# A two-block transformer layer on one core: attention and RWKV chunk products on zero-padded operands over the whole array

## Chip, cores and metric

One core of one Trainium2 chip runs the whole program. The metric is the device time of one execution in microseconds (us).

## What is computed

The first block runs attention and an RWKV-7 time mix side by side on 256 tokens of width 2048, then `w_out` and a gated FFN; a second block with three other attentions and an FFN follows. What the change touches is the first block's mix:

```python
def rwkv7_step(state, inp):                 # 16 heads of 64, scanned over 256 tokens
    r, w, k, v, a, bb = inp
    sa = jnp.einsum('bhij,bhj->bhi', state, a)
    state = (state * w[:, :, None, :] + sa[..., None] * bb[:, :, None, :]
             + v[..., None] * k[:, :, None, :])
    y = jnp.einsum('bhij,bhj->bhi', state, r)
    return state, y
...
kk = kk / jnp.maximum(jnp.sqrt(jnp.sum(kk * kk, axis=-1, keepdims=True)), 1e-12)   # per head
y = ((y - mu) * lax.rsqrt(var + GN_EPS)).reshape(b, s, RWKV_WIDTH) * ln_w + ln_b    # per head
...
logits = jnp.einsum('bnqrhd,bnkrhd->bnrhqk', qb, kc) * ATTN_SCALE + bias            # dilated attention
```

All inputs, weights and the result are float32.

## The kernel before, in words

Every large projection goes through `lin`: a 512 KB piece of weights is loaded on the SP queue (tile `raw`), ScalarE casts it to a high part `wh` (L333), VectorE subtracts for the low part `wl` (L334), and TensorE does three products per piece and token half, `wh·xh`, `wl·xh` and `wh·xl`, 512 columns wide (in the first projections 256). All of TensorE's products have the line L220 (helper `mm`) or L225 (helper `tr`, transposes), so they are told apart by their tiles.

Between these products the RWKV part is worked off in four groups `g` of four heads (two pairs `p` of two heads `hh`), and 256 tokens are cut into 8 chunks `c` of 32. Per group: `rwkv_pre` (decays; `lora`), `rwkv_keys` (`hs`, `nt`, `sp`: unit keys), `rwkv_rv` (`bn`), `rwkv_pairs` (products within the chunks `D`, transposed keys `BT`, values with tokens on partitions `V`), `solve_T` and `chain`, then `rwkv_out` (`yt` turns Y back to channels on partitions, `g` is the gate).

`solve_T` inverts the chunks' triangular matrices. `D` goes to DRAM and back in another layout (`scN`, `N`, on SP's queue), GpSimd does 31 steps of two operations each (tiles `X`, `T`, L584 and L586), the result goes to DRAM and back (`scT`, `TTx`), and only then can the first T product of that group's `chain` run.

`chain` goes from chunk to chunk: X = N·V + A·S, copied out of PSUM (`Xc`), U = T·X, copied (`UV`), the new state from `BKT`·UV (`S`), and Y = R·S + D·UV. Each float32 product appears as two MATMUL records, a transpose as one. A·S, R·S and the D products address 64 columns of the array, N·V and the T products 64 rows by 64 columns, `V` 64 by 32 and `yt` 128 by 64.

The attention (`attn_quarter`, 4 heads each) transposes q and k (`qkt`), forms logits of heads of 64 channels (`lg`) and works on tiles from a ring of 6 (`aq`). Loads for it and for the groups (`nq`, `toep`, `kB` ...) are issued by GpSimd.

A scheduler in the build fixes each engine's order once; on the chip every engine runs its list in that order, and an instruction that waits holds all behind it on its engine.

Of the kernel before, what the change touches and what calls it, by code (L numbers as in the profile page):

```python
# [19 lines left out]
P = 128  # L20
S = 256
# [76 lines left out]
def constants():  # L98
# [4 lines left out]
    # chunk mask: row (X, hh, t), column (Y, hh, s)  # L103
# [8 lines left out]
    c["selT"] = (np.arange(4)[:, None] == (np.arange(256) // 64)[None, :]).astype(f)  # L112
# [23 lines left out]
def host_arrays(inp):  # L136
    """Layout only: weights in the order of their use, parameters by channel."""
# [48 lines left out]
class Builder:  # L186
# [55 lines left out]
    def rstd(self, ss, n, eps, name):  # L242
        """(ss / n + eps) ** -0.5 for a small tile ss."""
# [16 lines left out]
    def row_rstd(self, ss, name):  # L260
        """Per-token rstd [128, tb] of rows of 2048, from the partial sums of squares."""
# [5 lines left out]
    def split_T(self, src, kts, hi, lo, gain=None, scale=None, tag="rw"):  # L267
        """hi + lo = (natural src(tb, kt) [128 tokens, 128 channels] transposed) * gain(kt)."""
# [31 lines left out]
    def lin(self, wname, bi, xT, evac, kmap=None, ks=None):  # L300
        """One block of columns of x @ w: evac(tb, psum [128 tokens, n]) for both token blocks."""
# [49 lines left out]
class Block1(Builder):  # L351
# [1 line left out]
    def rwkv_consts(self):  # L353
# [4 lines left out]
        self.selT = self.load_const("c_selT", [4, 256], pool)  # L358
# [27 lines left out]
    def slot(self, shape, name):  # L386
        """A tile of up to 2112 bytes per partition from the shared slots."""
# [14 lines left out]
    def nat_evac(self, dst, scale):  # L402
        """Evacuation of a projection block into dst[:, tb, :n], times the tokens' scale."""
# [5 lines left out]
    def shift_mix(self, out, ps, col):  # L409
        """out = ps + (ps of the token before - ps) * mix, [rows, 256]."""  # L410
# [22 lines left out]
    def lora_tanh(self, dst, r0, bias, st):  # L433
        """dst = tanh((bias + low rank) / 2)."""
        ps = self.aux("lora")
        for p in range(2):
            q = 2 * st.g + p
            self.mm(ps[:, p * S:(p + 1) * S], st.lup[r0:r0 + 64, p * P:(p + 1) * P], self.waT[r0:r0 + 64, :])
# [11 lines left out]
    def rwkv_pre(self, g):  # L450
        """What needs the low-rank inputs only: decays and the removal's strength."""
# [4 lines left out]
        st.lup = self.set2("lup", [P, S])  # L456
        nc.sync.dma_start(st.lup, self.A["lup"][:, cs])
        # decays, their inverses, and the products of both within a chunk (entry 0: the empty product)
# [17 lines left out]
        self.lora_tanh(st.a, 64, self.a0h, st)  # L476
        return st

    def rwkv_keys(self, st, natk):
# [4 lines left out]
        # half the removal key, of unit length per head  # L484
# [18 lines left out]
        nT = self.p1.tile([4, S], F32, tag="nT", name=self.nm("nT"))  # L503
        v.tensor_scalar(nT, pn[0:4, 0:S], 0.5, None, op0=ALU.mult)
# [14 lines left out]
    def rwkv_rv(self, st, natr, natv):  # L519
# [8 lines left out]
        # bonus, times v, in place of r  # L528
# [7 lines left out]
    def rwkv_pairs(self, st):  # L536
        """Decayed keys, products within the chunks, operands with tokens on partitions."""
# [22 lines left out]
        for p in range(2):  # L560
            pv = self.aux("V")
# [4 lines left out]
            nc.scalar.copy(st.UV[64:128, 8 * p:8 * p + 8, :], pv[64:128].rearrange("p (a b) -> p a b", a=8))  # L566

    def solve_T(self, st):
        """TTx = ((I - N)^-1)^T of every head and chunk, N the strictly lower products of the removal.

        Partition 32q + (head, chunk) holds the rows 4a + q of T."""
# [17 lines left out]
        r = 64 * (st.g % 2)  # L589
        for hh in range(2):  # L590
            nc.sync.dma_start(self.TTx[r + 32 * hh:r + 32 * hh + 32, :, 32 * hh:32 * hh + 32],
                         self.scT[hh].rearrange("c t s -> t c s"))

    def chain(self, st):
        """From chunk to chunk: X = A S + N_k V, U = T X, the state, and the outputs Y."""
# [10 lines left out]
        for c in range(8):  # L606
            for p in range(2):
                o, cs = 8 * p + c, slice(64 * p, 64 * p + 64)
# [3 lines left out]
            X = self.p1.tile([P, 2, 64], F32, tag="Xc", name=self.nm("Xc"), bufs=2)  # L612
            nc.scalar.copy(X[tr], a2(ch[0:64, 0:128]))
            for p in range(2):
                self.mm(ch[0:64, 128 + 64 * p:192 + 64 * p], self.TTx[tr, 8 * p + c, :], X[tr, p, :])
            v.tensor_copy(UVv[0:64, :, c, :], a2(ch[0:64, 128:256]))
            if c < 7:
                for p in range(2):
                    self.mm(ch[:, 256 + 64 * p:320 + 64 * p], st.BKT[:, 8 * p + c, :], st.UV[:, 8 * p + c, :])
                Sn = self.p1.tile([P, 2, 64], F32, tag="S", name=self.nm("S"), bufs=2)  # L620
                l = lc[:, :, c, :].to_broadcast([P, 2, 64])
            for p in range(2):
                o, ys = 8 * p + c, ch[64:128, 64 * p:64 * p + 64]
# [10 lines left out]

    def rwkv_out(self, st):
        """Group norm per head, back to channels on partitions, bonus and gate; stored for w_out."""
# [15 lines left out]
        gup = self.p1.tile([P, 2, S], F32, tag="gup", name=self.nm("gup"))  # L652
        nc.sync.dma_start(gup[:, 0, :], self.A["gup"][0:P, cs])
        nc.sync.dma_start(gup[0:32, 1, :], self.A["gup"][P:160, cs])
        ps, pg = self.aux("yt"), self.aux("g")
        for p in range(2):
            for c in range(4):
                for hh in range(2):
# [3 lines left out]
            self.mm(pg[:, p * S:(p + 1) * S], gup[:, 0, cs], self.gT[:, 0, :], stop=False)  # L662
            self.mm(pg[:, p * S:(p + 1) * S], gup[0:32, 1, cs], self.gT[0:32, 1, :], start=False)
            nc.scalar.activation(out[:, p, :], ps[:, p * S:(p + 1) * S], AF.Identity,
                                 scale=self.pv("ln_w", 2 * st.g + p), bias=self.pv("ln_b", 2 * st.g + p))
# [640 lines left out]
```

## Time and profile before

| | us |
|---|---|
| three runs | 2868.22, 2868.26, 2871.14 (median 2868.26) |
| profiled execution, span from first to last instruction | 2868.2 |
| TensorE busy with matmuls | 2824.0 (98%), 14032 records |
| VectorE, ScalarE, GpSimd busy | 1728.1, 1540.2, 165.4 |

The profiled execution's own time is its span; it stands within 0.1 us of the median. Records of matmuls overlap in the profile (each one's end is modelled), so what a product costs is read from the starts of neighbouring records, or from the chain of waits, which lays the pieces end to end. The first block's mix fills the first 667 us; after that come the FFNs and the second block, which the change leaves alone.

### The profile page before, as it was taken

The page shows a single profiled execution, that of the slowest core. Times are in us where ns is not written, and L with a number is a line of the kernel's source. Part 1 is how long each engine was busy: PE and PEld are TensorE (multiplying, and loading weights), DVE is VectorE, ACT ScalarE, POOL GpSimd, SP SyncE. Part 2 cuts the span into 40 slices and gives each one's busy share as a digit, 9 for nine tenths or more (in the row PEclk, how much of TensorE's full clock was granted, in tenths as well). Part 3 has the DMA queues.
Part 4 walks back from the last instruction along what each step waited for, and adds up shares of the span by engine and source line. Part 5 has one row for each costly group of instructions (what it writes and reads, how often), then busy time and mean ns, then how long its engine had stood idle before and what let it go on. Part 6 is the DMA issues. An engine that isn't in the chain of part 4 may idle for free.

```text
span 2868.2 us, 40953 instructions
## 1 busy us (share of the span) xinstructions
PE 2824.0 (98%) x14032; PEld 2327.4 (81%) x14032; DVE 1728.1 (60%) x3036; ACT 1540.2 (54%) x2791; POOL 165.4 (6%) x353
## 2 busy tenths in 40 slices
PE   7999999999999999999999999999999999999999
PEld 6877777777888888888888888888888888888887
DVE  5565656646555555555666676656666666667554
ACT  5444446446455454445555665555556666666444
POOL 1044033300000000000000000000000000000000
PEclk9999999999999999999999999999999999999999
DMA  6645446565555555555655545665555555555564
GB/s 215 193 160 153 159 158 202 182 197 191 188 192 186 191 191 189 191 192 187 214 186 173 169 165 191 202 202 195 190 184 186 186 185 185 184 184 190 200 201 167
DMA packets 168481, 534.43 MB, mean 186 GB/s; under 512 B 30853, under 2 KB 35983, under 8 KB 168272
## 3 DMA queue, kind: packets, MB, share of 16 engines
q1 hardware_dynamic: 149220, 487.91, 51.8%
q0 software_dynamic: 7360, 25.28, 2.9%
q10 hardware_dynamic: 11692, 18.63, 1.9%
q8 instruction: 110, 1.80, 0.3%
q14 instruction: 99, 0.81, 0.1%
HBM read 518.07 MB, written 16.82 MB: 186 GB/s over the span
## 4 chain that ended last, share of the span: by engine, by line
PE 93%; DMA 2%; DVE 1%; POOL 1%; ACT 1%; issue 1%; SPq 0%; ACTq 0%; DVEq 0%; POOLq 0%
PE lin L220 85%; PE ch L220 3%; PE tr L225 1%; PE uT L225 1%; POOL T L586 1%; POOL X L584 1%; DMA raw<-in_w_in_dram 1%; DVE wl L334 0%; PE o L220 0%; PE pt L220 0%; PE D L220 0%; PE lg L220 0%; PE V L220 0%; DMA x<-in_x_dram 0%; ACT wh L333 0%
## 5 line engine op out<-in xcount | busy, mean ns | idle before, releaser
L334 DVE TENSOR_TENSOR wl<-raw,wh 128x512 fp32r<-128x512 f32 (+2 forms) x1848 | 1268.4, 689 | 928.3 <-PE lin L220 814.2
L333 ACT CAST wh<-raw 128x512 fp32r<-128x512 f32 (+2 forms) x1848 | 1140.1, 619 | 1119.0 <-PE lin L220 1063.1
L220 PE MATMUL lin<-wl,x2h 128*128 128x512 f32 (+2 forms) x800 | 293.4, 369 | 2.9 <-DVE wl L334 2.9
L220 PE MATMUL lin<-wh,x2l 128*128 128x512 f32 (+2 forms) x800 | 289.4, 364 | 0.0
L220 PE MATMUL lin<-wl,u2h 128*128 128x512 f32 x704 | 281.0, 399 | 0.0
L220 PE MATMUL lin<-wl,hhi 128*128 128x512 f32 x704 | 275.0, 391 | 0.0
L220 PE MATMUL lin<-wh,u2l 128*128 128x512 f32 x704 | 274.3, 390 | 0.0
L220 PE MATMUL lin<-wl,uh 128*128 128x512 f32 x704 | 273.9, 391 | 0.0
L220 PE MATMUL lin<-wh,hlo 128*128 128x512 f32 x704 | 273.9, 389 | 0.0
L220 PE MATMUL lin<-wh,ul 128*128 128x512 f32 x704 | 272.7, 390 | 0.5 <-DVE ul L292 0.5
L220 PE MATMUL lin<-wh,x2h 128*128 128x512 f32 (+2 forms) x800 | 245.0, 365 | 1.6 <-ACT wh L333 1.2
L220 PE MATMUL lin<-wh,uh 128*128 128x512 f32 x704 | 227.6, 391 | 0.9 <-ACT uh L291 0.8
L220 PE MATMUL lin<-wh,u2h 128*128 128x512 f32 x704 | 225.5, 392 | 0.0
L220 PE MATMUL lin<-wh,hhi 128*128 128x512 f32 x704 | 219.9, 389 | 0.0
L220 PE MATMUL lin<-wl,xh 128*128 128x512 f32 (+2 forms) x512 | 188.8, 373 | 3.6 <-DVE wl L334 3.6
L220 PE MATMUL lin<-wh,xl 128*128 128x512 f32 (+2 forms) x512 | 178.3, 352 | 0.0
L220 PE MATMUL lin<-wh,xh 128*128 128x512 f32 (+2 forms) x512 | 156.0, 360 | 20.5 <-ACT wh L333 20.5
L220 PEld LDWEIGHTS lin<-wl,x2h 128*128 128x128 f32 x800 | 150.8, 189 | 29.0 <-DVE wl L334 6.0
L220 PEld LDWEIGHTS lin<-wh,x2h 128*128 128x128 f32 x800 | 147.9, 189 | 26.7 <-ACT wh L333 2.3
L220 PEld LDWEIGHTS lin<-wh,x2l 128*128 128x128 f32 x800 | 150.9, 189 | 22.7
L220 PEld LDWEIGHTS lin<-wh,uh 128*128 128x128 f32 x704 | 132.2, 188 | 29.4 <-ACT uh L291 1.5
L220 PEld LDWEIGHTS lin<-wh,u2h 128*128 128x128 f32 x704 | 132.2, 188 | 27.8
(417 smaller groups left out, 3754.4 us busy)
## 6 DMA issues: line engine op xcount, KB each, us to landing
raw<-in_w_in_dram SPq DMA_DIRECT2D x268, 512.0 KB, 3.8
raw<-in_w_gate_up_dram SPq DMA_DIRECT2D x176, 512.0 KB, 4.3
raw<-in_w_down_dram SPq DMA_DIRECT2D x176, 512.0 KB, 4.2
raw<-in_w_up_dram SPq DMA_DIRECT2D x176, 512.0 KB, 3.2
raw<-in_w_out_dram SPq DMA_DIRECT2D x64, 512.0 KB, 3.7
raw<-in_w_mem_kv_dram SPq DMA_DIRECT2D x16, 512.0 KB, 4.0
raw<-in_w_br_fox_dram SPq DMA_DIRECT2D x12, 512.0 KB, 3.2
raw<-in_w_br_sb_dram SPq DMA_DIRECT2D x12, 512.0 KB, 3.8
```

Source lines behind the costliest of these rows:

```text
L220: self.nc.tensor.matmul(out, lhsT=lhsT, rhs=rhs, start=start, stop=stop)
L225: self.nc.tensor.transpose(out, in_, self.ident[p0:p0 + n, p0:p0 + n])
L333: nc.scalar.copy(wh[:, :m * n], raw[:, cs])
L334: nc.vector.tensor_tensor(wl[:, :m * n], raw[:, cs], wh[:, :m * n].bitcast(F32), op=ALU.subtract)
L584: gp.tensor_tensor(x, T[:, 0:m, u:u + 1].to_broadcast([P, m, n]), N[:, u:u + 1, u + 1:32].to_broadcast([P, m, n]), op=ALU.mult)
L586: gp.tensor_tensor(w, w, x, op=ALU.add)
```

## The change

- `V`: 64 float32 products of 64x32 per group pair become four full 128x128 transposes per group; the copies out go by 32 partitions, four on ScalarE, four on VectorE. The half of `UV` that is not yet known is set to zero by GpSimd.
- `yt`: 16 float32 products per group become four transposes; four ScalarE copies and two VectorE operations take the place of two ScalarE activations.
- `rwkv_keys`: two narrow transposes, a VectorE operation and two products with a 4-row operand (`nt`, `nT`, `sp`) become a ScalarE copy `nr` [128, 512] and four transposes.
- `chain`: A·S and R·S are one product over all 128 columns, N·V comes with a D product over all rows and columns; T·X of both pairs is one product with a block-diagonal 128x128 `TTx`. X and U are copied in halves, one on VectorE and one on ScalarE. GpSimd copies U into `Ux` (rest zero), and D·Ux adds U's part to Y. Every chunk now waits for a GpSimd copy.
- `TTx` is one buffer for all groups (two halves before), filled by four DMAs in place of two; `lup` and `gup` are single zero-padded buffers; `qz` holds q zero-padded per head, one buffer, and the ring `aq` has 5 tiles.

```diff
 # rwkv_keys
-        pn = self.aux("nt")
-        for tb in range(2):
-            self.tr(pn[0:4, tb * P:(tb + 1) * P], nn[:, 4 * tb:4 * tb + 4])
...
+        nr = self.slot([P, 8, 64], "nr")
+        nc.scalar.activation(nr, nn.unsqueeze(2).to_broadcast([P, 8, 64]), AF.Copy, scale=0.5)
...
         for p in range(2):
-            self.mm(ps[:, p * S:(p + 1) * S], self.selT[:, p * P:(p + 1) * P], nT)
+            for tb in range(2):
+                self.tr(ps[:, p * S + tb * P:p * S + (tb + 1) * P], nr[:, tb, p * P:(p + 1) * P])
 # rwkv_pairs
-                for c in range(8):
-                    self.tr0(pv[64 + 32 * hh:96 + 32 * hh, c * 64:(c + 1) * 64],
-                             st.v[64 * hh:64 * hh + 64, p, c * 32:(c + 1) * 32])
+        nc.gpsimd.memset(st.UV[0:64], 0.0)
+        for i in range(4):
+            self.tr(pv[:, i * P:(i + 1) * P], st.v[:, i // 2, (i % 2) * P:(i % 2 + 1) * P])
...
 # solve_T
+        for p in range(2):
+            for hh in range(2):
+                r = slice(64 * p + 32 * hh, 64 * p + 32 * hh + 32)
+                nc.sync.dma_start(self.TTx[r, :, r], self.scT[hh, 8 * p:8 * p + 8].rearrange("c t s -> t c s"))
 # chain, per chunk c
-                self.mm(ch[0:64, cs], D[64:128, o, 0:64], st.UV[64:128, o, :], stop=(c == 0))
-                if c:
-                    self.mm(ch[0:64, cs], ARx[:, o, 0:64], S0[:, p, :], start=False)
-            nc.scalar.copy(X[tr], a2(ch[0:64, 0:128]))
-                self.mm(ch[0:64, 128 + 64 * p:192 + 64 * p], self.TTx[tr, 8 * p + c, :], X[tr, p, :])
-            v.tensor_copy(UVv[0:64, :, c, :], a2(ch[0:64, 128:256]))
+            if c:
+                for p in range(2):
+                    self.acc(xy[p], ARx[:, 8 * p + c, :], S0[:, p, :], start=(p == 0))
+                self.acc(xy[p], D[:, 8 * p + c, :], UV[p], start=(c == 0 and p == 0))
+            v.tensor_copy(X[0:64], xy[0][0:64])
+            nc.scalar.copy(X[64:128], xy[1][0:64])
+            self.acc(ch[:, 128:192], self.TTx[:, c, :], X)
+            v.tensor_copy(UV[0][0:64], ch[0:64, 128:192])
+            nc.scalar.copy(UV[1][0:64], ch[64:128, 128:192])
...
-                if c:
-                    self.mm(ys, ARx[:, o, 64:128], S0[:, p, :], stop=False)
-                self.mm(ys, D[:, o, 64:128], st.UV[:, o, :], start=(c == 0))
+            nc.gpsimd.tensor_copy(Ux[0:64], by(st.UV)[0:64, :, c, :])
+                self.acc(xy[p], D[:, 8 * p + c, :], Ux[:, p, :])
 # rwkv_out
-                    self.mm(ps[64 * hh:64 * hh + 64, p * S + c * 64:p * S + c * 64 + 64], st.Y[:, c, p, :],
-                            self.ident.rearrange("p (c h s) -> p h c s", c=2, h=2)[:, hh])
+            self.tr(ps[:, c * P:(c + 1) * P], st.Y[:, c].rearrange("p a i -> p (a i)"))
 # attn_quarter
-                self.mm(ps[:, 0:256], qT[r, h2, P:S], kT[r, h2, :])
+                self.mm(ps[:, 0:256], qz[:, h2, i, P:S], kT[:, h2, :])
```

TensorE's list, chunk 3 of group 0, products of `lin` left out (`ch` is the chain's PSUM bank, rows that end in x2 are a product per pair of heads). Before, from the T product to the Y products of the same chunk:

```order
L220 MATMUL ch_1700<-Xc_1757,TTx 64x64 x2
...
L220 MATMUL ch_1700<-UV_967,BKT_966 128x64 x2
L220 MATMUL ch_1700<-S_1745,ARx_398 64x64
L220 MATMUL ch_1700<-UV_967,D_965 64x64
...
L220 MATMUL ch_1700<-S_1764,ARx_398 64x64
L220 MATMUL ch_1700<-UV_967,D_965 64x64
```

Now:

```order
L648 MATMUL ch_1687<-Xc_1746,TTx 128x64
L219 MATMUL lora_3108<-waT,lup 128x256
...
L648 MATMUL ch_1687<-UV_975,BKT_974 128x64 x2
...
L648 MATMUL ch_1687<-Ux_403,D_973 128x64 x2
...
L648 MATMUL ch_1687<-S_1754,ARx_396 128x64 x2
L648 MATMUL ch_1687<-UV_975,D_973 128x64 x2
```

The Y products read `Ux` and stand behind the `BKT` products, six `lin` products further on here, right behind them in many other chunks; the next chunk's A and R come in one.

GpSimd's list at the same place, inside `solve_T` of group 1 (now; before, no row of `chain` stood on this engine):

```order
L594 TENSOR_TENSOR X_1909<-T_1908,N_1903 128x64
L636 COPY Ux_403<-UV_975 64x128
L596 TENSOR_TENSOR T_1908<-T_1908,X_1909 128x4x16
...
L596 TENSOR_TENSOR T_1908<-T_1908,X_1909 128x7x5
L636 COPY Ux_402<-UV_975 64x128
L594 TENSOR_TENSOR X_1909<-T_1908,N_1903 128x28
```

The copies of chunks 3 and 4 of group 0 now stand between the operations of group 1's `solve_T`: 31 of them are ahead of the first copy, 23 lie between the two. In TensorE's list 66 `lin` products (512 wide) and 28 others stand between the last `D` products of group 1 and the product that reads the first of these copies, then 30 and 7 up to the next. In group 2's `solve_T` the copies of chunks 6 and 7 of group 1 stand in the same way (16 and 28 operations) and a zeroing of `UV` behind them; in group 3's those of chunks 4 to 6 of group 2, 16 operations ahead of the first.

TensorE's list from the last `D` products of group 2 to that group's first T product, `lin` left out. Before there were 140 `lin` products in it, with 16 of V and all of yt among these rows:

```order
L220 MATMUL D_3469<-ARx_398,BKx 128x128 x4
...
L220 MATMUL V_3483<-k_c_ident,v_3267 32x64 x16
...
L220 MATMUL V_3501<-k_c_ident,v_3267 32x64 x16
...
L225 MATMUL nt_3876<-k_c_ident,knn_3863 4x128 x2
...
L220 MATMUL sp_3881<-nT_3879,k_c_selT 128x256 x2
L220 MATMUL yt_3919<-k_c_ident,Y_3282 64x64 x8
...
L225 MATMUL qkt_5055<-k_c_ident,nk_5043 128x128 x2
L220 MATMUL ch_3978<-Xc_3981,TTx 64x64 x2
```

Now there are 139, and yt stands later:

```order
L219 MATMUL D_3430<-ARx_396,BKx 128x128
...
L224 MATMUL V_3445<-k_c_ident,v_3226 128x128 x4
...
L648 MATMUL ch_3242<-Ux_403,D_1836 128x64 x2
L648 MATMUL ch_3909<-UV_3393,D_3391 128x64 x2
L224 MATMUL sp_3819<-k_c_ident,nr_3817 128x128 x4
L224 MATMUL qkt_4961<-k_c_ident,nk_4949 128x128 x4
L648 MATMUL ch_3909<-Xc_3912,TTx 128x64
```

Between the same two points TensorE has as many `lin` products as before and less small work. In group 0 the stretch has 153 in place of 144, and 24 narrow ones (256 columns) fewer stand ahead of its first `D`.

## Rows read from the trace of the kernel before

**Rows 1.** The page's head and its first part: busy time, share of the span and instructions of each engine; and from its groups VectorE's subtraction for `lin` (busy us, mean ns of one, idle before).

```profile
span 2868.2 us, 40953 instructions
PE 2824.0 (98%) x14032; PEld 2327.4 (81%) x14032; DVE 1728.1 (60%) x3036; ACT 1540.2 (54%) x2791; POOL 165.4 (6%) x353
...
L334 DVE TENSOR_TENSOR wl<-raw,wh 128x512 fp32r<-128x512 f32 (+2 forms) x1848 | 1268.4, 689 | 928.3 <-PE lin L220 814.2
```

**Rows 2.** Who TensorE waited for over the whole span: total us, times, longest.

```profile
PE lin L220 <- ACT wh L333: 23.4, 8, 15.3
PE qkt L225 <- DMA nq<-sp_q: 2.9, 1, 2.9
...
PE ch L220 <- DVE UV L616: 0.9, 2, 0.4
```

**Rows 3.** Busy time by stretch (us from the start, length, busy time and records of PE, PEld, DVE, ACT, POOL, then granted clock as a share of 2.4 GHz, DMA share, GB/s).

```profile
133.00:143.00 10.00, 10.00 (x75) 8.47 (x74) 1.54 (x3) 2.83 (x5) 0.74 (x1) 0.52 0.63 191
...
172.00:186.00 14.00, 11.08 (x41) 7.76 (x39) 6.57 (x12) 4.61 (x10) 4.61 (x13) 0.76 0.44 120
186.00:391.00 205.00, 204.70 (x1213) 157.42 (x1212) 119.31 (x244) 92.64 (x195) 36.13 (x80) 1.00 0.47 151
391.00:442.00 51.00, 49.18 (x302) 36.80 (x301) 36.76 (x75) 26.83 (x48) 31.52 (x70) 1.00 0.57 172
442.00:568.00 126.00, 126.00 (x803) 100.89 (x803) 78.65 (x181) 72.41 (x179) 40.57 (x89) 1.00 0.61 194
568.00:584.00 16.00, 13.74 (x69) 10.22 (x67) 6.39 (x14) 4.60 (x11) 2.89 (x5) 0.68 0.40 126
```

**Rows 4.** TensorE's timeline: start, us, what, records merged, and in brackets an idle time ahead of it.

```profile
126.61 1.05 PE L220 MATMUL D<-ARx,BKx 128*128 128x128 f32 x8
...
133.63 5.77 PE L220 MATMUL V<-k_c_ident,v 64*32 64x64 f32 x64
...
185.76 0.44 PE L220 MATMUL ch<-Xc,TTx 64*64 64x64 f32 x4
...
390.05 1.05 PE L220 MATMUL D<-ARx,BKx 128*128 128x128 f32 x8
...
437.08 0.69 PE L220 MATMUL yt<-k_c_ident,Y 128*64 128x64 f32 x16
...
441.64 0.41 PE L220 MATMUL ch<-Xc,TTx 64*64 64x64 f32 x4 [0.69 <-DMA TTx<-scT]
```

**Rows 5.** The chain of waits through the stretch 388 to 445: start, us, what (pieces laid end to end, so their lengths are what each took on the path).

```profile
390.21 0.89 PE D L220 x8
...
392.49 0.37 PE ch L220 x4
...
394.38 1.71 PE V L220 x32
396.08 0.61 PE ch L220 x8
...
436.75 2.10 DMA scT<-T
...
439.29 2.21 DMA TTx<-scT
```

**Rows 6.** The same view, 100 to 215.

```profile
103.56 2.65 PE lin L220 x22
...
130.97 7.14 DMA scN<-D
...
200.52 0.44 PE BT L225 x4
...
201.85 1.00 PE ch L220 x12
202.85 2.53 PE lin L220 x10
```

**Rows 7.** The same view, 560 to 590.

```profile
569.11 1.04 PE ch L220 x8
```

**Rows 8.** TensorE's timeline, 316 to 331, at full clock.

```profile
316.91 1.13 PE L220 MATMUL sp<-nT,k_c_selT 4*128 4x256 f32 x4
```

**Rows 9.** GpSimd's groups over the span: count | busy us, mean ns of one | idle before, and what ended it.

```profile
L584 POOL TENSOR_TENSOR X<-T,N 128x60 f32<-128x60 f32 (+24 forms) x124 | 51.3, 414 | 32.5 <-DMA N<-scN 23.7
L586 POOL TENSOR_TENSOR T<-T,X 128x60 f32<-128x60 f32 (+24 forms) x124 | 48.6, 392 | 9.1
L724 POOL DMA_DIRECT2D toep<-toepd x8 | 5.9, 734 | 63.4 <-PE pt L225 36.6 <-DMA toepd<-biasd 25.6 <-PE zt L225 0.9
```

**Rows 10.** GpSimd's timeline, 221 to 436: two operations of `solve_T` of group 1, then the first and the last one of group 2.

```profile
230.38 0.30 POOL L584 TENSOR_TENSOR X<-T,N 128x63 f32<-128x63 f32 x1
...
235.50 0.63 POOL L584 TENSOR_TENSOR X<-T,N 128x64 f32<-128x64 f32 x1
...
400.70 0.23 POOL L584 TENSOR_TENSOR X<-T,N 128x31 f32<-128x31 f32 x1 [0.77 <-DMA N<-scN]
...
434.27 0.54 POOL L586 TENSOR_TENSOR T<-T,X 128x8 f32<-128x8 f32 x1
```

**Rows 11.** SP's timeline, 434 to 442: the DMA issues that bring the solved matrices out and back.

```profile
434.83 2.53 SPq L588 DMA_DIRECT2D scT<-T  x4
438.90 0.88 SPq L591 DMA_DIRECT2D TTx<-scT  x2
```

More of the change, by code (lines that the diff above doesn't have):

```diff
@@ L377, in rwkv_consts @@
         self.BKx = pool.tile([P, 16, P], F32, tag="BKx", name="BKx")
-        self.TTx = pool.tile([P, 16, 64], F32, tag="TTx", name="TTx")
-        for t in (self.first, self.ARx[0], self.BKx, self.TTx, self.ARx[1]):
+        self.TTx = pool.tile([P, 8, P], F32, tag="TTx", name="TTx")
+        self.lup = pool.tile([P, 2, S], F32, tag="lup", name="lup")
+        self.gup = pool.tile([P, 2, S], F32, tag="gup", name="gup")
+        self.Ux = [pool.tile([P, 2, 64], F32, tag=f"Ux{i}", name=f"Ux{i}") for i in range(2)]
+        self.qz = pool.tile([P, 2, 2, S], F32, tag="qz", name="qz")
+        for t in (self.lup, self.first, self.ARx[0], self.BKx, self.TTx, self.gup, *self.Ux, self.ARx[1], self.qz):
             nc.gpsimd.memset(t, 0.0)
@@ L437, in lora_tanh @@
             q = 2 * st.g + p
-            self.mm(ps[:, p * S:(p + 1) * S], st.lup[r0:r0 + 64, p * P:(p + 1) * P], self.waT[r0:r0 + 64, :])
+            self.mm(ps[:, p * S:(p + 1) * S], self.lup[:, i, p * P:(p + 1) * P], self.waT)
             self.nc.scalar.activation(dst[:, p, :], ps[:, p * S:(p + 1) * S], AF.Tanh, scale=0.5, bias=bias[:, q:q + 1])
@@ L455, in rwkv_pre @@
         cs = slice(S * g, S * g + S)
-        st.lup = self.set2("lup", [P, S])
-        nc.sync.dma_start(st.lup, self.A["lup"][:, cs])
+        for i in range(2):
+            r = slice(64 * i, 64 * i + 64)
+            nc.sync.dma_start(self.lup[r, i, :], self.A["lup"][r, cs])
         sg = self.slot([P, 2, S], "sg")
@@ L559, in rwkv_pairs @@
                                 st.D[32 * hh:32 * hh + 32, :, 32 * hh:32 * hh + 32])
-        for p in range(2):
-            pv = self.aux("V")
-            for hh in range(2):
-                for c in range(8):
-                    self.tr0(pv[64 + 32 * hh:96 + 32 * hh, c * 64:(c + 1) * 64],
-                             st.v[64 * hh:64 * hh + 64, p, c * 32:(c + 1) * 32])
-            nc.scalar.copy(st.UV[64:128, 8 * p:8 * p + 8, :], pv[64:128].rearrange("p (a b) -> p a b", a=8))
+        nc.gpsimd.memset(st.UV[0:64], 0.0)
+        pv = self.aux("V")
+        for i in range(4):
+            self.tr(pv[:, i * P:(i + 1) * P], st.v[:, i // 2, (i % 2) * P:(i % 2 + 1) * P])
+        for j in range(4):
+            src = pv[32 * j:32 * j + 32].rearrange("p (a h i) -> p h a i", a=4, h=2)
+            for hh in range(2):
+                dst = st.UV[64 + 32 * hh:96 + 32 * hh, j::4, :]
+                if hh:
+                    v.tensor_copy(dst, src[:, hh])
+                else:
+                    nc.scalar.copy(dst, src[:, hh])
     def solve_T(self, st):
@@ L588, in solve_T @@
             nc.sync.dma_start(self.scT.rearrange("h c t s -> (h c) t s")[:, q::4, :], T[32 * q:32 * q + 32])
[L589 to L592, printed above, removed]
+        for p in range(2):
+            for hh in range(2):
+                r = slice(64 * p + 32 * hh, 64 * p + 32 * hh + 32)
+                nc.sync.dma_start(self.TTx[r, :, r], self.scT[hh, 8 * p:8 * p + 8].rearrange("c t s -> t c s"))
     def chain(self, st):
@@ L633, in chain, with acc @@
             S0 = Sn
+    def acc(self, out, lhsT, rhs, start=False):
+        self.nc.tensor.matmul(out, lhsT=lhsT, rhs=rhs, start=start, stop=True, skip_group_check=True)
     def rwkv_out(self, st):
@@ L655, in rwkv_out @@
         ps, pg = self.aux("yt"), self.aux("g")
+        for c in range(4):
+            self.tr(ps[:, c * P:(c + 1) * P], st.Y[:, c].rearrange("p a i -> p (a i)"))
+        src = ps.rearrange("p (c h t) -> p h c t", h=2, t=32)
         for p in range(2):
-            for c in range(4):
-                for hh in range(2):
-                    self.mm(ps[64 * hh:64 * hh + 64, p * S + c * 64:p * S + c * 64 + 64], st.Y[:, c, p, :],
-                            self.ident.rearrange("p (c h s) -> p h c s", c=2, h=2)[:, hh])
             cs = slice(p * P, (p + 1) * P)
[L662 to L665, printed above, removed]
+            for i in range(2):
+                self.mm(pg[:, p * S:(p + 1) * S], gup[:, i, cs], self.gT[:, i, :], start=(i == 0), stop=(i == 1))
+            for hh in range(2):
+                nc.scalar.copy(out[64 * hh:64 * hh + 64, p, :].rearrange("p (c t) -> p c t", t=32),
+                               src[64 * p:64 * p + 64, hh])
+            v.tensor_scalar(out[:, p, :], out[:, p, :], self.pv("ln_w", 2 * st.g + p), self.pv("ln_b", 2 * st.g + p),
+                            op0=ALU.mult, op1=ALU.add)
         v.tensor_tensor(out, out, st.bv, op=ALU.add)
@@ L695, in aq @@
         return self.p1.tile([P, w], F32, tag="aq%d" % w, name=self.nm(name), bufs={512: self.NAQ, 768: self.NAL}[w])
-    NAQ = 6
+    NAQ = 5
     NAL = 2
@@ L711, in attn_quarter @@
         natv = nat[2]
-        qT, kT = q2(self.aq("qT")), q2(self.aq("kT"))
-        for dst, n in ((qT, nat[0]), (kT, nat[1])):
+        kT, qz = q2(self.aq("kT")), self.qz
+        for i, n in enumerate(nat[:2]):
             ps = self.aux("qkt", "at")
@@ L717, in attn_quarter @@
                     self.tr(ps[:, j * S + tb * P:j * S + (tb + 1) * P], n[:, tb, j * P:(j + 1) * P])
-            nc.scalar.copy(dst, q2(ps))
+            if i:
+                nc.scalar.copy(kT, q2(ps))
+            else:
+                for h in range(2):
+                    nc.scalar.copy(qz[64 * h:64 * h + 64, :, h, :], q2(ps)[64 * h:64 * h + 64])
         on = self.aq("on")
```

28 lines of the change are left out of this document (12 added, 16 removed).

## The prediction, made before the run

> **What bounds the kernel now.** I read the page's busy shares first, then whom TensorE waits for, then the stretches of the first block, then the chain of waits inside them. TensorE is busy 98% of 2868.2 us [rows 1], and its waits on others are few: 23.4 us for `wh`, 15.3 of it at the start, and hardly 1 us for the chain's own copies [rows 2]. By stretches it has no idle time to speak of from 186 to 391 and from 442 to 568 [rows 3]. So in those two stretches a microsecond of work taken from TensorE's list is a microsecond off the end. That does not hold where something else sets the next event. From the last `D` products of group 0 (126.61) to its first T product (185.76), and from those of group 2 (390.05) to its first T product (441.64), the way leads through DRAM, GpSimd's 62 operations and DRAM again; at 441.64 TensorE itself waits 0.69 us for that way's end [rows 4]. Work taken out there only turns into waiting. The profiled execution's own time, its span of 2868.2 us, is within 0.1 us of the median, so no correction is made.
>
> **Prices of the pieces**, from starts or from pieces on the path. V: 1.71 us for 32 records [rows 5], 3.4 a group; four whole-array transposes like `BT` take 0.44 [rows 6]: -3.0 a group. yt: 0.69 for 16 records [rows 4], 1.4 a group against 0.44: -0.9. sp: 1.13 [rows 8], with the two narrow transposes 1.3 against 0.44: -0.85. A chunk: N·V and A·S 1.04 for 8 records [rows 7], T 0.37 for 4 [rows 5], BKT, R·S and D·UV 1.00 for 12 [rows 6], together 2.4. After, a chunk has nine products of two records each, 18. A whole-array record of 128 columns takes 0.11 (`BT`, and `D` at 0.89 for 8 [rows 5, 6]); products of 64 columns could be cheaper, down to the 0.076 of the eight records at 396.08 [rows 5], or as dear as the 0.13 of the octet [rows 7]. That bounds a chunk between 1.4 and 2.3; I take 0.115, 2.07, since the nearest whole-array rows are `BT` and `D`: -0.33 a chunk.
>
> What rows show here is that these eight small records side by side take 0.61 us, but the octet ahead of the T product 1.04 [rows 5, 7]. The Trainium skill, "TensorEngine Tiling (Array Packing)", section Overview, says the opposite of this change: operands of at most 64 rows or columns leave the array half used, and independent tiles of it give up to 2x or 4x. That is a rival below; by the octet's row the tiles of the old form gave little of it.
>
> **The change, stretch by stretch.**
> - Up to the last `D` of group 0: 24 narrow `lin` products fewer stand ahead, 0.12 each (2.65 for 22 [rows 6]): **-2.9**.
> - From there to group 0's first T product: V takes 5.77 us here [rows 4], at a granted clock of 0.52 [rows 3], and almost all of that goes; but the stretch is set by the way through GpSimd (scN alone 7.14 [rows 6]; in group 2 scT 2.10 and TTx 2.21 besides GpSimd's 34 from 400.70 to 434.81 [rows 5, 10]), so nothing is gained. `TTx` is filled by four transfers in place of two, 0.44 us each on SP's queue [rows 11]: **+0.9**. More idle time than now may come in front of the T product.
> - 186 to 391: V of group 1 -3.0, sp of group 2 -0.85, yt of group 0 -0.95, 15 chunks -5.0: -9.8. Against it stand two waits for GpSimd. N of group 1 arrives some 10 us after its last `D` (390.21+0.89 to 400.70 in group 2 [rows 5, 10]); then 31 operations at 0.40 busy [rows 9] and about 0.07 between them, 14.6, and the copy of chunk 3, up to 0.65: ready at some 25. TensorE has 66 `lin` at 0.25 [rows 6] and 28 others in between, 22 to 23: a wait of 2. To chunk 4 it is 23 operations, 11, against 30 `lin` and seven others, 9: another 2. **-5.8** in all.
> - 391 to 441.6: work of V, yt and chunks goes from a stretch that the way through GpSimd sets (nothing gained). Two more copies and the zeroing of `UV` lie between the operations, each from 0.23 to 0.65 as the operations are [rows 10], and two more `TTx` issues: **+2**. TensorE is idle longer there; as after the idle time near 172 to 175, when it waited 2.9 for `nq` [rows 2] and the granted clock over 172 to 186 was 0.76 [rows 3], a dip of 14 x 0.24 = 3.4 us is possible; I put **+1.7** for an even chance.
> - 442 to 667: V of group 3 -3.0, yt of groups 2 and 3 -1.8, that of group 1, which moves in here, +0.4, 16 chunks -5.3: -9.7. In 568 to 584, where the chain runs with short waits and no `lin` beside it, the clock was 0.68 [rows 3], 16 x 0.32 = 5.1 us lost; with the order changed and fewer records I take half back, -2.5. The copies of chunks 4 to 6 of group 2 stand in group 3's `solve_T`, with loads of memory, `mixd` and `toep` ahead of some; by the same reckoning as above, two waits of 2: +4. **-8.2**.
>
> Taken at nothing: `lora`, `g` and `lg` on zero-padded rows (as many columns as before; the cover is that a record's time went with columns, see `D` against the octet, else up to +0.02 a record); the split X and U copies and the copies of V and yt (VectorE is 60% busy, ScalarE 54% [rows 1], and the U copies cost TensorE 0.9 in all before [rows 2]; if the later of the two engines is late by 0.1 each chunk, +3); the ring of 5 for 6 and the single `qz` and `lup` (TensorE's one wait for attention's loads was 2.9 [rows 2], which could come a second time).
>
> Sum: -2.9 + 0.9 - 5.8 + 2.0 + 1.7 - 8.2 = -12.3, so **2856 us**. The bounds of a chunk (1.4 and 2.3, over the 31 chunks that count) would move the sum by -21 and +7, waits of none to 20 us by -8 and +12; both ends together are unlikely, and I give this case 2842 to 2866.
>
> How long a copy takes is not shown; in rows of nearly one size GpSimd's operation took 0.30 once and 0.63 another time [rows 10], and VectorE's subtraction takes 0.69 [rows 1]. The Trainium skill, "SBUF — State Buffer", section SBUF: two separate sides, says that a VectorE operation with two SBUF inputs and a GpSimd operation that reads SBUF take one port pair in turn, each for its whole instruction; the two rows fit that without proving it, and by it a copy could last 0.3 to 1.0 and the 32 copies up to 22 us more than their shortest, which counts only beyond their cover.
>
> **Rivals.**
> 1. All of TensorE's saved work comes back. The list's pieces fall by V 12, yt 3.8, sp 3.4, 32 chunks 10.6 and narrow `lin` 2.9: 32.7 us, so 2835, and 2830 with the dip of 568 to 584 gone. For it: TensorE is the bound nearly everywhere. Against it: the 0.69 wait at 441.64 [rows 4] says that GpSimd's way closes the two stretches. Chance 0.17.
> 2. Slower: GpSimd's copies become the bound. Every D·Ux product has one ahead of it, and GpSimd's list holds issues that wait: 63.4 us in all for the eight `toep` issues alone, 36.6 of it for TensorE [rows 9]. If TensorE waits 1.4 us on average per chunk, 45 us stand against 32.7: 2880. The point from which it decides is 1.0 us a chunk. Against it: in most chunks 12 `lin` products, 3 us [rows 6], lie between the T product and the D·Ux product. Chance 0.12.
> 3. Side by side: if the old small records overlapped so that each cost 0.076 [rows 5], a chunk cost 24 x 0.076 = 1.83 and the new one 0.24 more: 31 chunks +7.4 in place of -10.2, so 2874. The octet at 1.04 [rows 7] speaks against it. Chance 0.03. (It is what the rule of the Trainium skill on tiling, quoted above, would do here.)
> 4. No change to speak of: savings land in the two stretches that GpSimd's way sets, and waits for `Ux` eat the rest, 2863 to 2872. Chance 0.13.
>
> **How the numbers follow.** The forecast's case has 0.55. A measurement of this kernel can tell 0.2%, 5.7 us, from no change: faster is below 2862.5. The forecast's case lies there but for 0.03, rival 1 wholly: 0.52 + 0.17 = 0.69. Same: 0.03 + 0.13 = 0.16. Slower, rivals 2 and 3: 0.15. The range takes in the forecast's case, half of rival 1 and nearly all of rival 4: 2834 to 2870.
>
> **What would show it.** V, yt and sp as four records of 0.11 each and a chunk of about 2.07 are the savings' test; a chunk above 2.4 refutes the sum. First T products near 184 and, counted from group 2's last `D`, 53 us later would show that GpSimd's way sets both stretches; well under 50 speaks for rival 1. TensorE's waits on `Ux` should sum to about 8 us and lie at chunks 3 and 4 of group 0 and 4 to 6 of group 2; over 32 us is rival 2. The clock over the stretch of 568 to 584, then some 12 us earlier, and behind the second T wait decides 2 us each way. The prediction is wrong if the end of the first block does not move by about what the whole time moves, since the second block is untouched.

## The result, and the profile after

The changed kernel takes 2852.85 us (median of four runs) against 2869.70: ratio 0.9942, 95% interval 0.9928 to 0.9956. The profiled executions have spans of 2850.1 and 2868.2, 18.1 apart. (A run's time stands some 1.8 above its span: the profiled run of the changed kernel took 2851.9. So the span of 2868.2 is a run of some 2870, not one within 0.1 of the median; the medians are 16.9 apart.) In the list of `lin` products, from number 2200 on, just behind the first block, the two traces stay 18.0 us apart to the end, so everything happened in the first block.

TensorE's timeline of the changed kernel; the rows answer to [rows 4]:

```profile
123.66 1.05 PE L219 MATMUL D<-ARx,BKx 128*128 128x128 f32 x8
...
179.44 0.43 PE L648 MATMUL ch<-Xc,TTx 128*128 128x64 f32 x2 [0.57 <-DMA TTx<-scT]
...
227.79 1.12 PE L648 MATMUL ch<-Ux,D 128*128 128x64 f32 x4 [3.29 <-POOL Ux L636]
...
368.07 0.39 PE L219 MATMUL D<-ARx,BKx 128*128 128x128 f32 x2
...
390.25 0.66 PE L648 MATMUL ch<-Ux,D 128*128 128x64 f32 x4 [3.29 <-POOL Ux L636]
...
422.58 0.66 PE L648 MATMUL ch<-Xc,TTx 128*128 128x64 f32 x2 [2.66 <-DMA TTx<-scT]
...
642.02 0.73 PE L219 MATMUL lin<-wh,mixh 128*128 128x512 f32 x2 [3.15 <-ACT wh L332]
```

Read against [rows 4, 5], this gives the sum's stretches. The last `D` of group 0 starts 2.95 us earlier, group 0's first T product 6.3; the end of group 2's last `D` (391.1 before, 368.5 now) comes 22.6 earlier, group 2's first T product 19.1; the rest gives 1.0 back. The brackets show what took it: two waits for `Ux`, one for `TTx` behind GpSimd's way, one ahead of the last `w_out` products.

The same in whole stretches, cut in both traces at the same `lin` products (numbers 650, 1350, 1750 and 2200). Columns as in [rows 3]. Before:

```profile
0.00:118.89 118.89, 98.44 (x714) 92.10 (x715) 69.26 (x149) 66.03 (x150) 13.00 (x24) 0.97 0.64 202
118.89:397.19 278.30, 272.84 (x1586) 210.50 (x1585) 153.84 (x306) 124.61 (x253) 65.97 (x150) 0.97 0.52 161
397.19:550.39 153.20, 151.38 (x915) 119.00 (x914) 104.65 (x227) 88.45 (x201) 72.09 (x159) 1.00 0.62 194
550.39:701.57 151.18, 143.80 (x757) 110.83 (x756) 87.53 (x178) 73.99 (x149) 7.22 (x12) 0.97 0.58 187
```

After:

```profile
0.00:120.71 120.71, 98.22 (x724) 93.54 (x725) 73.86 (x150) 66.40 (x151) 16.96 (x32) 0.97 0.66 204
120.71:369.55 248.84, 234.41 (x1263) 197.15 (x1261) 154.78 (x321) 128.08 (x271) 70.11 (x165) 0.97 0.59 174
369.55:533.72 164.17, 146.49 (x782) 122.58 (x780) 106.33 (x244) 92.08 (x222) 75.57 (x169) 0.96 0.60 185
533.72:683.60 149.88, 137.27 (x669) 112.05 (x668) 92.84 (x198) 76.85 (x166) 9.94 (x21) 0.97 0.59 189
```

Length less TensorE's busy time is idle time; busy time times (1 - granted clock) is what the clock lost; the rest is work at full clock. Summed over the four rows: before, 35.1 idle, 15.5 clock, 651.0 work; after, 67.2, 20.0 and 596.4 (the clock has two digits and is the mean over idle time too, so there are some 3 us of doubt in the last two). **TensorE has some 55 us less to do, and 32 of them came back as idle time, a few more through the clock.** The third stretch even became 11 us longer: its idle time grew from 1.8 to 17.7.

Where the work went is told by the chain of waits, 590 to 625, in group 3's chain; here one chunk is T 0.17, BKT and D·Ux 0.84, and the next chunk's A and R and N·V 0.84, 1.85 us together:

```profile
607.98 0.17 PE ch L648 x2
...
610.97 0.84 PE ch L648 x8
...
613.71 0.84 PE ch L648 x8
```

Times from each record to the next, idle time left out, summed by tile up to `lin` number 2200: the chain 76.6 to 56.1, V 16.1 to 1.8, yt 5.8 to 1.8, sp with nt 5.5 to 1.5, `lora` 9.4 to 5.3, `g` 9.9 to 7.1, the logits 10.6 to 10.2 (the clock's loss included).

And whom TensorE waits for now (total us, times, longest), to set beside [rows 2]; before, `wl` had 6.5 and `TTx` 0.7, and there was no wait for `kA`, `nk` or `BKT`:

```profile
PE lin L219 <- ACT wh L332: 25.3, 7, 15.3
PE lin L219 <- DVE wl L333: 13.4, 17, 1.8
PE ch L648 <- POOL Ux L636: 8.1, 3, 3.3
PE zt L224 <- DMA kA<-sp_kA: 4.5, 1, 4.5
PE qkt L224 <- DMA nk<-sp_k: 3.6, 3, 2.8
PE ch L648 <- DMA TTx<-scT: 3.2, 2, 2.7
PE qkt L224 <- DMA nq<-sp_q: 2.6, 2, 1.7
PE BT L224 <- ACT BKT L561: 2.2, 1, 2.2
```

No one wait is the give-back: `Ux` adds 8 us, `wl` 7, the loads `kA` and `nk` 8 together, and `TTx`, `BKT` and `wh` some 2 each; `nq` adds nothing.

### The profile page after: what moved, and what is told of

Same layout as the page of the kernel before. It is cut to its first block, busy times and chain, and to the rows that moved or that the text cites. A ratio compares the mean times of both kernels' runs of the same rounds, so it can differ in the third digit from the quotient of the medians.

```text
span 2850.1 us, 40071 instructions
## 1 busy us (share of the span) xinstructions
PE 2773.8 (97%) x13496; PEld 2320.1 (81%) x13496; DVE 1741.2 (61%) x3088; ACT 1550.3 (54%) x2847; POOL 179.7 (6%) x395
## 3 DMA queue, kind: packets, MB, share of 16 engines
q1 hardware_dynamic: 149404, 487.90, 54.7%
## 4 chain that ended last, share of the span: by engine, by line
PE 89%; DMA 4%; POOL 2%; issue 2%; DVE 2%; ACT 1%; SPq 0%; ACTq 0%; DVEq 0%; POOLq 0%
PE lin L219 83%; PE ch L648 1%; POOL T L596 1%; POOL X L594 1%; PE tr L224 1%; PE uT L224 1%; DMA scN<-D 1%; DMA N<-scN 1%; DVE wl L333 0%; DMA x<-in_xT_dram 0%; PE o L219 0%; PE D L219 0%; DMA raw<-in_w_out_dram 0%; DMA mem<-in_memT_dram 0%; PE lg L219 0%
## 5 line engine op out<-in xcount | busy, mean ns | idle before, releaser
L219 PEld LDWEIGHTS lin<-wh,x2l 128*128 128x128 f32 x800 | 150.9, 189 | 22.8
```

What stands on the lines that cost most here:

```text
L219: self.nc.tensor.matmul(out, lhsT=lhsT, rhs=rhs, start=start, stop=stop)
```

## The experiments

All ratios are to the kernel before, with 95% intervals; the last three columns are the sums over the four stretches as above, from each profiled execution. The kernel before ran again beside each set of runs, with medians from 2869.6 to 2873.2, so kernels of different sets are compared by their ratios.

| kernel | us | ratio | idle | clock | work |
|---|---|---|---|---|---|
| before | 2869.7 | 1 | 35.1 | 15.5 | 651.0 |
| changed | 2852.9 | 0.9942 (0.9928-0.9956) | 67.2 | 20.0 | 596.4 |
| a1 V, yt, sp only | 2860.7 | 0.9962 (0.9948-0.9975) | 45.0 | 15.7 | 630.0 |
| a2 chain only | 2864.6 | 0.9972 (0.9962-0.9982) | 47.9 | 23.2 | 625.9 |
| a3 Ux on VectorE | 2837.1 | 0.9877 (0.9863-0.9892) | 59.3 | 13.2 | 597.8 |
| b1 Ux on ScalarE | 2854.6 | 0.9929 (0.9913-0.9945) | 66.7 | 13.0 | 598.0 |
| b2 a3, tail shared | 2842.6 | 0.9895 (0.9879-0.9910) | 62.6 | 16.6 | 599.9 |
| b3 a3, rest unpadded | 2856.5 | 0.9940 (0.9925-0.9955) | 55.1 | 26.3 | 606.4 |
| b4 before, grouped | 2866.6 | 0.9978 (0.9970-0.9987) | 39.5 | 14.1 | 644.5 |
| c1 half of solve_T | 2840.4 | 0.9888 (0.9875-0.9900) | 57.0 | 16.9 | 598.3 |
| c2 a3, loads on SP | 2855.1 | 0.9931 (0.9917-0.9946) | 69.5 | 22.8 | 593.4 |
| d1 solve_T on VectorE | 2841.6 | 0.9908 (0.9893-0.9923) | 59.0 | 13.4 | 601.5 |
| d2 a3 and d1 | 2837.6 | 0.9887 (0.9874-0.9901) | 56.5 | 17.6 | 595.3 |

Every edit is scheduled anew by the build, so two kernels differ in their order too. The work column hardly feels that (593 to 602 in all kernels that have the whole new form); idle time and clock do, and no run holds the order fixed, so a few us of either can be the order's. The profiled execution of b1 is 7 us faster than its median, that of b2 6 us slower; the others stand within 3.1.

**a1, a2: the change in two parts.** a1 takes over the new `rwkv_keys`, `V` and `yt`; a2 the new `chain`, the `TTx` transfers, `Ux` and the zeroing of `UV`.

> V, yt and sp by whole-array transposes alone, the chain as it was. Theory 1 (TensorE's saved work counts except between the last D of groups 0 and 2 and their first T products, and what the whole change gives back it gives back through GpSimd's list): V of groups 1 and 3 -6, yt -3, sp -2.5, and no wait for Ux: 12 us less than before, about 2857, and TensorE waits on POOL Ux do not exist. Rival A (the transposes' extra copies on ScalarE and VectorE make the closing group's way to w_out longer and take most of it back): within 5 us of before, with a wait ahead of the last w_out products of 3 us or more.

> The chain's change alone (merged A.S/R.S, N.V through D, shared T, Ux on GpSimd, TTx in four transfers), with V, yt and sp as before. Theory 1: chunk 2.4 to 1.85 us, 31 chunks -17, less some 8 us of waits for Ux and as much for loads behind them and half clock: 2858 to 2866. Rival B (the chain's change is the whole gain, the transposes give nothing): 2850 to 2855.

Both came out about where theory 1 said (11 and 8 us less by the ratios, no `Ux` wait in a1, 3.3 us of them in a2, less than expected); rivals A and B fall. In work a1 saves 21 and a2 25. That is 46 of the 55; b3 finds about the other 9. And a1 shows that idle time comes back without any copy on GpSimd: 10 us of it (45.0 against 35.1), most of it in waits for loads that before did not hold TensorE:

```profile
PE zt L225 <- DMA rB<-sp_rB: 6.0, 1, 6.0
PE zt L225 <- DMA kA<-sp_kA: 4.1, 1, 4.1
```

**a3, b1: another engine for the copy.**

```diff
-            nc.gpsimd.tensor_copy(Ux[0:64], by(st.UV)[0:64, :, c, :])
+            v.tensor_copy(Ux[0:64], by(st.UV)[0:64, :, c, :])        # a3
+            nc.scalar.copy(Ux[0:64], by(st.UV)[0:64, :, c, :])       # b1
```

> The changed kernel with the copy Ux on VectorE in place of GpSimd, nothing else. Theory 1 (GpSimd's list, in which the copies stand between solve_T's operations and the loads, takes the gain back): the 8.1 us of waits for Ux go, loads arrive earlier, 6 to 12 us less than the changed kernel's 2853: 2841 to 2847. Rival C (the waits come from the order in which loads are issued, not from Ux; VectorE is then late with wl instead): 2850 to 2857.

> The changed kernel with the copy Ux on ScalarE. Theory 1 (any engine but GpSimd will do, since it is the copies' place in GpSimd's list that costs): 2835 to 2843, like the copy on VectorE. Rival D (VectorE's faster copy is what helped; ScalarE already holds half of X and U, the copies for V, yt and k): 2846 to 2855.

a3 beats the changed kernel, and by more than forecast: 2837.1, twice the gain. b1 does not: theory 1's sharper form, any engine but GpSimd, falls, and the time is rival D's. TensorE's waits in a3, then in b1:

```profile
PE lin L219 <- ACT wh L332: 24.8, 8, 15.6
PE lin L219 <- DVE wl L333: 11.9, 15, 1.7
...
PE zt L224 <- DMA kB<-sp_kB: 4.1, 1, 4.1
```

```profile
PE lin L219 <- ACT wh L332: 28.9, 10, 15.4
...
PE qkt L224 <- DMA nq<-sp_q: 4.1, 2, 3.6
```

With the copy on VectorE the rows for `Ux` are gone and the wait for `wl` is no longer than in the changed kernel (11.9 against 13.4). The two profiled executions lie 13 us apart: 8 of it is idle time, which is what the waits for `Ux` had taken, and 5 to 7 is clock. The loads did not arrive earlier, as theory 1 had it: `kA`, `kB`, `rA` and `nq` still hold TensorE for 12.8. Whether the clock's part comes from the copy or from the new order is not shown.

On ScalarE the wait for `wh` grew from 25.3 to 28.9, and other loads are late instead; the idle time is that of the changed kernel (66.7). The copy itself takes 0.22 us on VectorE and 0.30 on ScalarE (medians), a difference of 2.5 us over all 32, so its speed alone does not decide. What else ScalarE holds, the other half of rival D, is the likelier reason, but no run shows it apart.

**b2: the tail.** Two of `rwkv_out`'s four copies on VectorE.

> Ux on VectorE, and in rwkv_out two of the four copies out of yt's bank on VectorE in place of ScalarE. Theory 2 (the 3.15 us ahead of the last w_out products is the way of group 3 through these copies, 1.5 us of ScalarE's in a row): the wait falls by 0.7 to 1.5 us, 1 us less than Ux on VectorE alone, 2836. Rival E (the wait is set by the other steps): 2837, wait still above 3.

The wait ahead of the last `w_out` products fell from 3.15 to 1.80, as theory 2 said (before the change it was 1.79), and rival E falls. The total did not follow: 2842.6. The intervals of b2 and a3 overlap, so whether b2 is slower at all is not shown; a gain of 1 us would not show either.

**b3: the padding of `lora`, `g` and the logits**, undone on a3 (`lup`, `gup`, `qT` and a ring of 6 as before).

> Ux on VectorE, and the zero-padding of lora, g and the logits undone (lup, gup and q as before, ring of 6 tiles); chain, V, yt and sp stay as changed. Theory 3 (these parts cost and give nothing but for short waits on nq and nk): 2834 to 2840. Rival F (whole-array rows there are worth as much per product as in the chain): 2845 or more, with lora, g and lg records longer.

Rival F holds: 2856.5, with 8.6 us more work than a3 (by tile, `lora` +4.2, `g` +4.5, logits +3.3, the clock's loss included; the chain, too, came out 4.7 longer) and 13 more lost through the clock. How much of those 13 belongs to the unpadded products and how much to the order is not settled.

**b4: why the old octet was dear** (the eight records of N·V and A·S ahead of a T product). The kernel before, with both N·V products first (the accumulation's marks are set otherwise, so what X sums differs; number and shapes of products don't).

```diff
-                self.mm(ch[0:64, cs], D[64:128, o, 0:64], st.UV[64:128, o, :], stop=(c == 0))
-                if c:
-                    self.mm(ch[0:64, cs], ARx[:, o, 0:64], S0[:, p, :], start=False)
+                self.nc.tensor.matmul(ch[0:64, cs], lhsT=D[64:128, o, 0:64], rhs=st.UV[64:128, o, :], start=True, ...)
+            for p in range(2 if c else 0):
+                o, cs = 8 * p + c, slice(64 * p, 64 * p + 64)
+                self.nc.tensor.matmul(ch[0:64, cs], lhsT=ARx[:, o, 0:64], rhs=S0[:, p, :], start=False, ...)
```

> The kernel before, with a chunk's two N.V products ahead of its two A.S products in place of one after the other by pair; no other change. Theory 4 (a record that follows one with another number of rows of the array pays some 0.14 us, so the old octet of 1.03 was dear because it changed rows at every pair of records): the octet falls to 0.7 to 0.8, 28 chunks 7 us, of which 4 to 6 count: 0.998 of before. Rival G (64-row records simply cost 0.13): octet still 1.0, 1.000 of before.

TensorE's timeline of one chunk, before and in b4; `64*64` and `128*64` are the rows and columns of the array that a record uses:

```profile
206.63 0.33 PE L220 MATMUL ch<-UV,D 64*64 64x64 f32 x2
206.89 0.33 PE L220 MATMUL ch<-S,ARx 128*64 128x64 f32 x2
207.15 0.32 PE L220 MATMUL ch<-UV,D 64*64 64x64 f32 x2
207.40 0.33 PE L220 MATMUL ch<-S,ARx 128*64 128x64 f32 x2
```

```profile
194.75 0.44 PE L609 MATMUL ch<-UV,D 64*64 64x64 f32 x4
195.12 0.45 PE L613 MATMUL ch<-S,ARx 128*64 128x64 f32 x4
```

Before, each pair of records takes 0.26 and the next has other rows; in b4 four in a row take 0.37. So two more records of the same form add 0.11, and each change of form some 0.15. The octet falls from 1.03 to 0.74, 28 of them 8.1 us; by tile the chain falls from 76.6 to 68.4, the work column says 6.5, the time 0.9978 (0.9970 to 0.9987). Theory 4 holds for a change between 64 and 128 rows; a change of the columns alone was not tried.

**c1: a shorter way through GpSimd**, on the changed kernel (`range(0, 31, 2)` for `range(31)` in `solve_T`, which leaves out half of the steps).

> The changed kernel, copies on GpSimd, with every second step of solve_T left out (32 operations per group in place of 62; the triangular inverse is not complete). Theory 5 (the way from the last D to the first T product through GpSimd, with 13.5 us of TensorE's idle time in its two stretches, and the copies held between its operations, 8.1 us, take back what the smaller list of TensorE gives): idle time falls by 12 to 20 us, 2833 to 2842. Rival H (once that way is shorter, ScalarE's and VectorE's lists or loads hold TensorE just as long): 2846 to 2853.

2840.4, inside theory 5's range, but with less idle time gone than it asked for: 67.2 to 57.0. Half of GpSimd's operations were worth 12 us by the medians, 15 by the ratios; 57 us of idle time are left, 15 of it the start. From the start of the last `D` to that of the first T product it is 41.7 us in group 0 and 36.0 in group 2, against 55.0 and 54.4 in the changed kernel, and the waits for `Ux` fall to 3.0. But the build's order puts fewer `lin` products into the shorter way (105 and 98 for 153 and 139), that is, less cover: less work for TensorE that hides the way. So TensorE still waits 3.3 and 0.9 at its end.

**c2: loads away from GpSimd**, on a3 (`nc.sync.dma_start` for `nc.gpsimd.dma_start` in the two loads).

> Ux on VectorE, and the loads of attention's q, k, v and of the groups' k, r, v issued on SP's queue in place of GpSimd's. Theory 6 (TensorE's waits on kA, rA, kB and nq, 12.6 us in the kernel with Ux on VectorE, come from the loads' places in GpSimd's list): 2827 to 2833. Rival I (they stand on stretches that the way to the first T product sets anyway, or hold up the weights on SP's queue): 2835 to 2845.

18 us more than a3 by the medians, 15 by the ratios, more than rival I allowed, and theory 6 falls. TensorE's waits, and SP's list ahead of the first of them:

```profile
PE qkt L224 <- DMA nq<-sp_q: 11.6, 2, 10.7
PE ch L648 <- DMA TTx<-scT: 10.4, 2, 10.2
```

```profile
173.27 2.59 SPq L598 DMA_DIRECT2D scT<-T  x4
175.91 0.61 SPq L726 DMA_DIRECT2D nq<-sp_q  x1
```

The load of `nq` stands behind `scT`, and SP held `scT` until GpSimd's last operation of `solve_T` ended at 173.24: on this queue the load waits for the way through GpSimd. At the second wait, ahead of group 2's first T product, it is not the loads that hold `TTx`: only two issues, 1.2 us, stand between `scT` and `TTx`. TensorE had 133 `lin` products to cover that way, 139 in a3, and ran out of work 10 us early. Both waits lie in the two stretches that GpSimd's way sets, from the last `D` to the first T product: TensorE idles for 13.9 and 10.2 us in them here and for 9.6 and 6.6 in a3.

**d1, d2: solve_T on VectorE** (`gp = nc.vector`), on the changed kernel and on a3.

> The changed kernel with solve_T's operations on VectorE and the copies Ux left on GpSimd, which then holds little but copies and loads. Theory 5 (GpSimd's list of solve_T's operations, copies and loads takes the gain back): waits for Ux gone, the way from D to the first T product shorter by 10 us or more, 2833 to 2842. Rival J (VectorE, 60% busy, is then late with wl and with the halves of X and U): waits on wl above 15 us, 2848 or more.

> Ux and solve_T's operations both on VectorE. Theory 5: shorter way to the T products on top of no Ux waits, 2825 to 2834. Rival J: VectorE becomes the late one, 2837 or more.

d1 is some 10 us faster than the changed kernel, as theory 5 said, with the copies still on GpSimd, but not for theory 5's reason. Rows of the waits, then the last `D` and the first T product of groups 0 and 2:

```profile
PE lin L219 <- DVE wl L333: 17.8, 21, 3.7
PE ch L648 <- POOL Ux L636: 2.1, 3, 1.3
```

```profile
123.03 1.05 PE L219 MATMUL D<-ARx,BKx 128*128 128x128 f32 x8
199.88 0.33 PE L648 MATMUL ch<-Xc,TTx 128*128 128x64 f32 x2
...
355.83 1.05 PE L219 MATMUL D<-ARx,BKx 128*128 128x128 f32 x8
418.29 0.33 PE L648 MATMUL ch<-Xc,TTx 128*128 128x64 f32 x2
```

The way from `D` to the T product did not become 10 us shorter; it became longer, 75.8 and 61.4 us from the last `D`'s end against 54.7 and 54.1 in the changed kernel. `solve_T` of group 0 took 47 us on VectorE and 32 on GpSimd. But the build's order put more `lin` products into it, 226 and 187 for 153 and 139, and neither of these T products waits any longer: d1's gain speaks for cover, not for a shorter way. The waits for `Ux` fell to 2.1 and are not gone. d2 is no faster than a3, which is rival J's number, and the waits for `wl` that rival J asked for are there in d1.

So taking the copies away from solve_T's operations (a3), solve_T away from the copies (d1), or half of solve_T (c1) gives 10 to 19 us by the ratios, and a3 and d1 together (d2) no more than a3 alone. That the copies' place among solve_T's operations costs TensorE time is shown by a3, for the 8 us of waits that go with it; c1 and d1 cut these waits too, but change the way and its cover at the same time and so don't single it out. It is not the only cause: between 56 and 59 us of idle time stay in these four, where the kernel before had 35, spread over VectorE, ScalarE and loads.

## Why the prediction was right, and where two of its terms were not

The time and the sign held: 2852.9 against 2856, and 16.9 us off the median, 18.1 off the span, against 12.3. So did the main mechanism: TensorE's saved work counts only where TensorE is the late one, and GpSimd's way and copies take part of it back. That the sum came out so near was luck as well, because two errors stood against each other, a saving 22 us too small and a give-back 17 us too small.

- **Up to the last `D` of group 0**: -2.95 against -2.9, partly by luck: TensorE's busy time fell by 5.0 there and its idle time grew by 2.0. (The narrow `lin` products were only moved behind that point; the number of `lin` products did not change.)
- **From there to the first T product**: -3.4 against +0.9. The step "set by the way through GpSimd, so nothing is gained" was too strict here: before, [rows 4] show no wait for `TTx` at 185.76, so TensorE was the later one; now it waits 0.57.
- **To the last `D` of group 2**: -16.3 against -5.8. The mis-sized term is the chunk: 1.85 in place of 2.07, so -0.55 and not -0.33 each (by tile the whole chain fell by 20.5, 0.64 a chunk). I took the price of a whole-array record from `BT` and `D`, with 128 columns moving; the chain's move 64. Here 1.6 chunks also moved behind the stretch's end: its chain records went from 344 to 228, at 24 and 18 a chunk. And `lora` and `g`, "taken at nothing", saved 6.9 us by tile in the whole block.
- **The waits for `Ux`**: 8.1 in all where I had about 8, but that is luck in part. The wait at chunk 3 of group 0 came as reckoned, 3.3 for 2, and one at chunk 4 of group 2, 1.5 for 2. The wait at chunk 4 of group 0 did not come, and another of 3.3 came at chunk 6 of group 1 (390.25), which I had not listed.
- **To the first T product of group 2**: +3.6 against +2.0, and TensorE idle ahead of it (2.66), as argued; from the last `D`'s end it is 54 us, near the 53 that was to show GpSimd's way. But the copies and the zeroing did not lengthen GpSimd's own part, 379.68 to 413.01 and 33.3 us against 34.1. The way grew ahead of it, where `N` came 11.2 us after the last `D`'s end in place of 9.6, and behind it, with `scT` and `TTx`, 9.6 in place of 6.8.
- **To the end**: +1.0 against -8.2 and the clock's +1.7. Some 14 us of work less were all given back, nearly all of it as idle time (7.4 before, 20.9 now). The step that failed is "two waits of 2": beside one wait for `Ux` there are waits for `wl`, `BKT`, `nq`, raw weights (2.60 at 630.7) and the way from group 3's `yt` through four ScalarE copies, three VectorE operations and the cast of `mixh` to the last products (3.15 at 642.0, 1.79 before; the bracket names `wh`, since ScalarE's next casts stood behind that of `mixh`), which I had covered by "VectorE is 60% busy".
- **The clock**: in the stretch of 568 to 584 the granted clock was 0.50, the level of 1.2 GHz, for 10.3 us before (572.7 to 583.0); now it is for 6.8 (554.7 to 561.5), so some 1.7 came back where I had 2.5. It is also 0.50 from 418.1 to 428.4, from within a wait of 2.85 for `nk` and across the one of 2.66 for `TTx`. TensorE was busy for 6.9 of these 10.3 us, so some 3.5 were lost where I had 1.7 for an even chance.
- **The whole**: the list lost some 55 us of work, not 33, and some 37 came back, not 20. Rival 1 (all comes back) had the size of the saving too small and its fate wrong. Rival 2's mechanism is real, at 0.25 us a chunk and not at 1.0. Rival 3, the side-by-side reading, is out for the chain: the old octet was dear, for a reason that b4 shows. It is not out everywhere. In the old logits the two heads of a pair used rows 0 to 63 and 64 to 127, and eight records in a row took 0.86, no longer than four (0.85, from 474.94 to 475.79). On zero-padded rows eight take 1.23 and four 0.66 (526.22 to 526.88): padding made the long runs dearer and the short ones cheaper, and the logits' total hardly moved. Before, then after:

```profile
527.22 0.93 PE L220 MATMUL lg<-kT,qT 64*128 64x256 f32 x8
528.08 0.50 PE L220 MATMUL lin<-wl,memh 128*128 128x512 f32 x1
```

```profile
513.08 1.47 PE L219 MATMUL lg<-kT,qz 128*128 128x256 f32 x8
514.31 0.48 PE L219 MATMUL lin<-wl,memh 128*128 128x512 f32 x1
```

## What to carry to other kernels

When the busiest engine sheds work in many small pieces, price the saving and the cover apart: each microsecond it saves is also a microsecond less of cover for every copy, load and hand-over that it hid. Shares of busy time (60%, 54%, 6%) say little about whether a copy of 0.4 us stands at the right place in its engine's list; look at what it stands behind. And before rows of small products are priced, see whether neighbouring records use the same rows of the array, and how many of one form stand in a row.

## What was not expected of the hardware

- A change between 64 and 128 rows from one record to the next cost about 0.15 us here (0.26 a pair when alternating, 0.37 for four of one form). The Trainium skill, "TensorEngine Tiling (Array Packing)", section Tiling Modes, says that changing the mode drains TensorE; b4 fits that, with this price. It is part of why zero-padding to whole-array products, with half of their operands zeros, was the cheaper form; for `V` and `yt` the number of records fell as well (64 to 4 and 32 to 4 a group). Two `lora` records between whole-array ones took 0.62 in the old form and 0.24 in the new one, from these starts (before, then after). Two changes make some 0.3 of that difference; no run sets the rest apart.

```profile
51.67 0.70 PE L220 MATMUL lora<-waT,lup 64*128 64x256 f32 x2
52.29 0.51 PE L220 MATMUL lin<-wh,xh 128*128 128x256 f32 x2
```

```profile
45.98 0.59 PE L219 MATMUL lora<-waT,lup 128*128 128x256 f32 x2
46.22 0.47 PE L219 MATMUL lin<-wl,xh 128*128 128x256 f32 x1
```

- A copy of 64x128 on GpSimd takes 0.39 us on average (32 of them), 0.28 at the shortest and 1.79 once, so all 32 took 3.3 us more than their shortest, not up to 22; but one was waited for up to 3.3, because of what stood ahead of it in GpSimd's list:

```profile
L636 POOL COPY Ux<-UV 64x128 f32<-64x128 f32 x32 | 12.3, 386 | 177.3 <-ACT UV L629 177.1
```
